# Plain fp32 state products and Newton reciprocal roots in the scan of a hybrid SSD and attention block

## The chip, the cores and the metric

The kernel runs on one core of one Trainium2 chip. The metric is the device time of one execution, in microseconds. Engines are named as in the profile: PE is TensorE, PEld its weight load, DVE is VectorE, ACT is ScalarE, POOL is GpSimd, SP is SyncE, which here only issues DMAs.

## What is computed

The reference is one encoder layer on 1024 tokens of width 1024, in float32. A combined projection feeds a bidirectional state-space scan (SSD) and a neighbourhood attention; their outputs go through one output projection and a squared-ReLU MLP. What the change touches is in these lines (cut):

```python
# ssd_chunked, once per direction, chunks of 128 tokens, 2 groups of 8 heads of 64
chunk_states = jnp.einsum("bclgn,bclgep->bcgepn", bc, xc * decay_to_end[..., None])
chunk_decay = jnp.exp(a_cum[:, :, -1])
def step(h, inp):
    s_c, d_c = inp
    return d_c[..., None, None] * h + s_c, h
_, h_in = lax.scan(step, h0, (...))
y_off = jnp.einsum("bclgn,bcgepn->bclgep", cc, h_in) * jnp.exp(a_cum)[..., None]
# ssd_mixer: gate and grouped RMSNorm over 512 columns
g = g * lax.rsqrt(jnp.mean(g * g, axis=-1, keepdims=True) + EPS)
# neighbourhood_attention: RMSNorm of q and k over each head's 64 columns
q = rmsnorm(q.reshape(bsz, t, NA_HEADS, NA_HEAD_DIM), q_norm_w) * (NA_HEAD_DIM ** -0.5)
k = rmsnorm(k.reshape(bsz, t, NA_HEADS, NA_HEAD_DIM), k_norm_w)
```

## The kernel before

The program is written tile by tile in Python; a planner orders the instructions of each engine ahead of the run, by the dependencies between tiles, the free buffers and its own estimate of each instruction's time. On the chip each engine then works through its list strictly in that order and waits, at the head of the list, for whatever is not ready.

Large products are made of three passes in a reduced fp32 format (fp32r): an operand is split into a high part, rounded by ACT, and a low part, the difference, taken by DVE or POOL; `mm3` (L177 to L180) multiplies high by high, high by low and low by high. The weights are split on their way in by `load_w` (ACT at L148, DVE or POOL at L149), values that come out of PSUM by `split_from_psum` (L184, L185; with a scale L187, L188).

The first part (up to about 275 us) norms and transposes the input (L210), projects x, B, C and dt, applies the convolution (`conv`, L448 to L484) and projects z, which goes through Silu (L509) to memory. The transposed B of each chunk is kept as split pair `bNh`, `bNl`; B and C by state row stay whole in `bT` and `cT`.

Then the scan is traced as a loop of eight steps `i` over two groups `g`, each with `backward(7 - i, g)` and `forward(i, g)`. `backward` also does the part within the chunk for both directions: C by B (`pcb`, L587), the decay matrices `rb` loaded by DMA, subtracted on POOL (L612), merged on DVE (L618), exponentiated on ACT (L623), multiplied by `pcb` on DVE (L625), and eight fp32 products `pd` on PE (L630). The outputs are added up in `y1`, on POOL (L638, L641, L649, L666) and DVE (L642). In both directions:

- `decay_state` weights x with the decay on POOL (`xw`, L653 and L672), splits it (`xh` L540 on ACT, `xl` L541 on DVE), multiplies it by the B of the chunk into `pS` (three passes), multiplies the state by its decay on POOL (L549), adds `pS` on DVE (L550) and splits the new state (`sh` L553 on ACT, `sl` L554 on DVE). `sh` and `sl` have one buffer per group, which both directions use in turn.
- `carried` splits the C of the chunk (`ch` L562, `cl` L563), multiplies it by the split state into `py` (three passes) and scales the result on DVE (`yo`, L567).
- `gated`, once per chunk and group, multiplies `y1` by the gate on DVE (L574), sums its squares on ACT (L576), takes the reciprocal root with `inv_rms`, scales on ACT (L578) and stores by a DMA from ACT's queue.

`pcb`, `pS` and `py` share two PSUM buffers ("s"); `rb` has two buffers, `yo` and `xw` one.

Behind the scan in the program, but independent of it and therefore mixed with it by the planner, stands the projection of q, k and v (`qkv_proj`, six weight blocks of eight token blocks, each 24 passes into `pq`, three PSUM buffers). For q and k `normed_split` squares on ACT (L695), sums on DVE (L697), takes the reciprocal root of 8 columns with `inv_rms`, scales on DVE (L699), transposes on PE (L705), splits (L187, L188) and stores with DMAs from ACT's queue.

`inv_rms` (L199 to L203) is two POOL instructions: mean plus epsilon (L201) and a power with the exponent -0.5 from the tile `half` (L202). It is called 32 times for q and k, 16 times in `gated`, 8 times before the MLP.

Later come the attention with the output projection mixed in (about 675 to 1050 us; L928 to L959), the MLP's first product (to about 1390 us) and its second.

## Time and profile before

| what | value |
|---|---|
| median of three runs | 1725.57 us (1724.66 to 1726.45) |
| the profiled execution | 1725.33 us |
| its span, first to last instruction | 1723.5 us |
| mean granted clock of PE | 0.98 |
| table loads of ACT, of 1283 ns each | 7, the last at 280.72 us (L623) |
| DMA traffic | 269.75 MB |

The profile is of one execution. A page of it gives busy time of each engine, the span in 40 equal slices (each digit the busy share in tenths), and the costliest groups of instructions; other views answer questions about a stretch of time, a tile or a source line, list what each engine waited for (total us, times, longest us), or the instructions in order of time (start, duration). Matmuls are pipelined, so their durations overlap and the distance between starts is what one costs. A weight load (PEld) and its matmul are two records.

### The profile page before, as it was taken

What the parts mean: (1) busy time and instruction counts of PE and PEld (TensorE: products, weight loads), DVE (VectorE), ACT (ScalarE), POOL (GpSimd) and SP (SyncE); (2) the same over time, 40 slices, a digit from 0 to 9 for tenths busy, and PEclk for the clock granted to TensorE, in tenths of its full rate; (3) what the DMA queues carried; (4) which work ended last, traced back from release to release, by engine and by line L of the source; (5) the groups of instructions that cost most, each with busy time, mean ns of one, the idle gap of its engine ahead of it and who ended that gap; (6) DMA issues with size and microseconds to landing.
All of it is one profiled execution on the core that took longest, in us unless ns stands there. A gap on an engine that the chain in (4) does not pass through costs nothing. (4 is left out here: it accounts for less than half of the span.)

```text
span 1723.5 us, 20879 instructions
## 1 busy us (share of the span) xinstructions
PE 1636.0 (95%) x7461; PEld 1304.6 (76%) x7461; DVE 1106.3 (64%) x1687; ACT 726.5 (42%) x1189; POOL 705.6 (41%) x496
## 2 busy tenths in 40 slices
PE   6999999989888999999999988999999978999999
PEld 5788888777766777777767767788888866888887
DVE  5767214889787744778787776454343359787863
ACT  5434223434344434555565533454444443333330
POOL 4000004888778741221242242244444426555551
PEclk9999999999998999999999999999999989999999
DMA  8213338876675796754453141254344394644231
GB/s 200 62 37 104 89 98 242 210 195 207 213 206 161 234 311 199 240 150 138 132 183 123 56 159 49 73 190 153 134 159 147 125 349 149 201 141 166 92 110 73
DMA packets 178499, 269.75 MB, mean 157 GB/s; under 512 B 13963, under 2 KB 105051, under 8 KB 178395
## 3 DMA queue, kind: packets, MB, share of 16 engines
q1 hardware_dynamic: 135419, 231.18, 42.6%
q10 hardware_dynamic: 42976, 37.23, 7.1%
q8 instruction: 59, 0.97, 0.2%
q14 instruction: 45, 0.37, 0.1%
HBM read 185.21 MB, written 86.50 MB: 158 GB/s over the span
## 5 line engine op out<-in xcount | busy, mean ns | idle before, releaser
L760 POOL TENSOR_TENSOR wl<-wraw,wh 128x1024 fp32r<-128x1024 f32 x110 | 300.1, 2740 | 350.1 <-ACT wh L759 336.7
L745 PE MATMUL px<-wh,ahl 128*128 128x512 f32 x512 | 163.7, 397 | 9.8 <-ACT ahl L759 9.8
L759 ACT ACTIVATE wh<-wraw 128x1024 fp32r<-128x1024 f32 x110 | 115.7, 1054 | 127.4 <-issue 42.4
L179 PE MATMUL pq<-wl,hTh 128*128 128x512 f32 x384 | 153.1, 400 | 4.6 <-DVE wl L149 4.4
L745 PE MATMUL px<-h,wh 128*128 128x512 f32 x496 | 156.5, 396 | 0.0
L178 PE MATMUL pq<-wh,hTh 128*128 128x512 f32 x384 | 153.1, 401 | 1.9 <-ACT wh L148 1.2
L180 PE MATMUL pq<-wh,hTl 128*128 128x512 f32 x384 | 151.9, 396 | 0.0
L759 ACT ACTIVATE ahl<-ar 128x1024 fp32r<-128x1024 f32 x56 | 58.9, 1053 | 173.0 <-PE px L745 89.6
L760 DVE TENSOR_TENSOR ahl<-ar,ahl 128x1024 fp32r<-128x1024 f32 x56 | 107.3, 1917 | 37.4 <-ACT ahl L759 36.2
L745 PEld LDWEIGHTS px<-wh,ahl 128*128 128x128 f32 x512 | 97.3, 190 | 31.9 <-ACT ahl L759 10.2
L745 PEld LDWEIGHTS px<-h,wh 128*128 128x128 f32 x496 | 93.4, 189 | 22.4
L149 DVE TENSOR_TENSOR wl<-wraw,wh 128x1024 fp32r<-128x1024 f32 x40 | 55.0, 1376 | 83.3 <-ACT wh L148 82.7
L878 POOL TENSOR_TENSOR mb<-braw,nam 128x256 f32<-128x256 f32 (+1 forms) x48 | 41.0, 884 | 159.7 <-DVE nmx L936 123.4
L184 ACT ACTIVATE pth<-ptp 128x384 fp32r<-128x384 f32 (+1 forms) x128 | 58.4, 459 | 107.8 <-PE ptp L959 106.8
L745 PE MATMUL px<-wl,ahl 128*128 128x512 f32 x256 | 100.9, 394 | 0.0
L745 PE MATMUL px<-h,wl 128*128 128x512 f32 x248 | 98.1, 396 | 0.0
L179 PEld LDWEIGHTS pq<-wl,hTh 128*128 128x128 f32 x384 | 73.2, 191 | 22.1 <-DVE wl L149 7.9
L149 POOL TENSOR_TENSOR wl<-wraw,wh 128x1024 fp32r<-128x1024 f32 x18 | 43.8, 2446 | 110.5 <-ACT wh L148 84.3
L745 PE MATMUL pz<-wh,ahl 128*128 128x512 f32 x256 | 82.8, 400 | 6.5 <-DVE acc L1330 5.0
L178 PEld LDWEIGHTS pq<-wh,hTh 128*128 128x128 f32 x384 | 72.9, 190 | 18.2 <-ACT wh L148 2.5
L180 PEld LDWEIGHTS pq<-wh,hTl 128*128 128x128 f32 x384 | 73.2, 191 | 14.7
L612 POOL TENSOR_TENSOR rb<-rb,c 128x512 f32<-128x512 f32 x64 | 75.0, 1192 | 21.5 <-DMA rb<-cum_dr 18.7
(265 smaller groups left out, 4242.6 us busy)
## 6 DMA issues: line engine op xcount, KB each, us to landing
act_dr<-cq SPq DMA_DIRECT2D x56, 512.0 KB, 3.0
ar<-act_dr SPq DMA_DIRECT2D x56, 512.0 KB, 3.8
wraw<-in_w_in_dram SPq DMA_DIRECT2D x44, 512.0 KB, 4.0
rb<-cum_dr SPq DMA_DIRECT2D x32, 512.0 KB, 7.6
wraw<-in_w_mlp_in_dram SPq DMA_DIRECT2D x32, 512.0 KB, 4.7
wraw<-in_w_mlp_out_dram SPq DMA_DIRECT2D x32, 512.0 KB, 5.3
q_dr<-hl ACTq DMA_DIRECT2D x64, 128.0 KB, 3.2
k_dr<-hl ACTq DMA_DIRECT2D x16, 512.0 KB, 3.2
```

Source lines behind the costliest of these rows:

```text
L149: lo_eng.tensor_tensor(lo[:, 0:n], raw[:, 0:n], hi[:, 0:n].bitcast(F32), op=sub)
L178: nc.tensor.matmul(pt, lhsT=ah, rhs=bh, start=first, stop=False)
L179: nc.tensor.matmul(pt, lhsT=ah, rhs=bl, start=False, stop=False)
L180: return nc.tensor.matmul(pt, lhsT=al, rhs=bh, start=False, stop=last)
L184: nc.scalar.activation(hi, src, AF.Copy)
L612: nc.gpsimd.tensor_tensor(rb[:, d], rb[:, d], c1[:, d, c, h0 : h0 + 4].unsqueeze(2).broadcast_to([P, 4, P]), op=sub,)
L745: nc.tensor.matmul(pt, lhsT=a, rhs=b, start=f, stop=l, skip_group_check=True)
L759: nc.scalar.activation(hl[0], src, AF.Copy)
L760: eng.tensor_tensor(hl[1], src, hl[0].bitcast(F32), op=sub)
L878: nc.gpsimd.tensor_tensor(mb[:, s].rearrange("p (s r c) -> p s r c", r=16, c=8), v[:, a:b], nam[:, s].rearrange("p (s r c) -> p s r c", r= ...
```

## The change

It has two parts. In the scan, the splits of B, of the weighted x, of the state and of C are left out, and each of the two products per chunk, group and direction is one plain fp32 matmul; the state has two buffers per direction and group and is read by PE itself; the first state of each is copied from PSUM by ACT instead of DVE. In the norms of `gated` and of q and k, `inv_rms` is replaced by a function of six instructions: mean plus epsilon on DVE, Ln and Exp with the scale -0.5 on ACT, and one Newton step in three DVE operations. An explicit instruction loads ACT's table number 6 behind the last Silu of z. The input norm and the norm before the MLP keep POOL's power.

```diff
+LN_EXP = 6
...
+    def inv_rms_newton(pool, ss, n, width, tag):
+        r = pool.tile([P, width], F32, tag=tag, name=tag, bufs=2)
+        nc.vector.tensor_scalar(ss, ss, 1.0 / n, EPS, op0=mul, op1=add)
+        nc.scalar.activation(r, ss, AF.Ln)
+        nc.scalar.activation(r, r, AF.Exp, scale=-0.5)
+        nc.vector.scalar_tensor_tensor(ss, ss, -0.5, r, op0=mul, op1=mul)
+        nc.vector.tensor_tensor(ss, ss, r, op=mul)
+        nc.vector.scalar_tensor_tensor(r, ss, 1.5, r, op0=add, op1=mul)
+        return r
...
-        bNh = sp.tile([P, NT, 2, P], F32R, name="bNh")
-        bNl = sp.tile([P, NT, 2, P], F32R, name="bNl")
+        bN = sp.tile([P, NT, 2, P], F32, name="bN")
...
-                        split_from_psum(bNh[s], bNl[s], pv)
+                        nc.scalar.copy(bN[s], pv)
...
-                    nc.scalar.activation(zs, pt, AF.Silu, scale=rcol[:, t : t + 1])
+                    last_silu = nc.scalar.activation(zs, pt, AF.Silu, scale=rcol[:, t : t + 1])
...
+            with tc.issue_after(last_silu.ins):
+                nc.scalar.add_instruction(
+                    mybir.InstLoadActFuncSet(
+                        act_func_set_id=LN_EXP,
...
             def decay_state(d, c, g, xw):
                 prev = st[d][g]
                 pS = ps_s("pS")
-                xh = qp.tile([P, 512], F32R, tag="xh", name="xh", bufs=1)
-                xl = qp.tile([P, 512], F32R, tag="xl", name="xl", bufs=1)
-                nc.scalar.activation(xh, xw, AF.Copy)
-                nc.vector.tensor_tensor(xl, xw, xh.bitcast(F32), op=sub)
-                mm3(pS, bNh[:, c, g, :], bNl[:, c, g, :], xh, xl, True, True)
-                new = prev and prev[0]
+                nc.tensor.matmul(pS, lhsT=bN[:, c, g, :], rhs=xw, start=True, stop=True)
+                new = qp.tile([P, 512], F32, tag=f"st{d}{g}", name="st", bufs=2)
                 if prev is None:
-                    new = qp.tile([P, 512], F32, tag=f"st{d}{g}", name="st", bufs=1)
-                    nc.vector.tensor_copy(new, pS)
+                    nc.scalar.copy(new, pS)
                 else:
                     dec = ed[:, d, c, 8 * g : 8 * g + 8]
-                    nc.gpsimd.tensor_tensor(h8(new), h8(new), hb(dec), op=mul)
+                    nc.gpsimd.tensor_tensor(h8(new), h8(prev), hb(dec), op=mul)
                     nc.vector.tensor_tensor(new, new, pS, op=add)
-                sh = qp.tile([P, 512], F32R, tag=f"sh{g}", name="sh", bufs=1)
-                sl = qp.tile([P, 512], F32R, tag=f"sl{g}", name="sl", bufs=1)
-                nc.scalar.activation(sh, new, AF.Copy)
-                nc.vector.tensor_tensor(sl, new, sh.bitcast(F32), op=sub)
-                st[d][g] = (new, sh, sl)
+                st[d][g] = new
...
-                ch = qp.tile([P, P], F32R, tag="ch", name="ch", bufs=2)
-                cl = qp.tile([P, P], F32R, tag="cl", name="cl", bufs=2)
-                nc.scalar.activation(ch, ct, AF.Copy)
-                nc.vector.tensor_tensor(cl, ct, ch.bitcast(F32), op=sub)
-                mm3(py, ch, cl, *st[d][g][1:], True, True)
+                nc.tensor.matmul(py, lhsT=ct, rhs=st[d][g], start=True, stop=True)
...
-                r = inv_rms(qp, ss, 512, 1, "ry")
+                r = inv_rms_newton(qp, ss, 512, 1, "ry")
...
-                r = inv_rms(hp, ss, HD, 8, "rq")
+                r = inv_rms_newton(hp, ss, HD, 8, "rq")
```

More of the change, by code (lines that the diff above doesn't have):

```diff
@@ L519, in hymba_block @@
             qp = p2.enter_context(tc.tile_pool(name="qs", bufs=2, side="right", reuse_waits="tile"))
+            with tc.issue_after(last_silu.ins):
+                nc.scalar.add_instruction(
+                    mybir.InstLoadActFuncSet(
+                        act_func_set_id=LN_EXP,
+                        name=nc.get_next_instruction_name(),
+                        engine=mybir.EngineType.Activation,
+                    )
+                )
             zt = qp.tile([P, 192], F32, tag="y1", name="zt")
```

## The prediction

> **What bounds the kernel now.** I read the page first, then the table of stretches, then the waits of TensorE and of VectorE in the one stretch where TensorE is not full, then the groups of instructions that the diff touches.
>
> ```profile
> PE 1636.0 (95%) x7461; PEld 1304.6 (76%) x7461; DVE 1106.3 (64%) x1687; ACT 726.5 (42%) x1189; POOL 705.6 (41%) x496
> ...
> PE   6999999989888999999999988999999978999999
> ...
> POOL 4000004888778741221242242244444426555551
> PEclk9999999999998999999999999999999989999999
> ```
>
> TensorE is the bound of nearly the whole span. Its longest stretch with gaps lies about the ninth to thirteenth slice (43 us each; eights among the nines), where POOL is at seven or eight tenths. This is where the scan runs, with the q, k and v projections filling TensorE between the scan's products. The stretches, with one from the attention behind it for comparison:
>
> ```profile
> 275.00:605.00 330.00, 297.61 (x1427) 237.95 (x1427) 262.32 (x382) 132.41 (x236) 263.74 (x243) 0.98 0.73 212
> 475.00:575.00 100.00, 85.81 (x384) 67.28 (x383) 80.07 (x111) 44.53 (x80) 82.10 (x77) 0.93 0.69 200
> 675.00:1000.00 325.00, 318.65 (x1542) 238.61 (x1539) 257.31 (x729) 179.22 (x448) 80.33 (x61) 0.98 0.49 153
> ```
>
> After each stretch and its length stand PE, PEld, DVE, ACT, POOL, then the granted clock. In the scan TensorE is idle for 330 - 297.6 = 32.4 us (9.8%), with DVE at 79% and POOL at 80%. In the attention DVE is at 79% too, but POOL at 25%, and TensorE is idle for 6.4 us only (2.0%). So a DVE at four fifths does not by itself starve TensorE; a POOL at four fifths beside it goes with gaps. What TensorE waits for, from 275 to 680 us, and what DVE waits for, from 275 to 605 us:
>
> ```profile
> PE pcb L587 <- DVE yo L567: 7.5, 4, 3.1
> PE pd L630 <- DVE rb L625: 7.3, 9, 1.3
> PE pq L179 <- DVE wl L149: 4.4, 5, 1.7
> PE py L178 <- DVE yo L567: 2.5, 2, 2.0
> ```
>
> ```profile
> DVE rb L618 <- POOL rb L612: 16.6, 15, 2.5
> DVE y L642 <- POOL y L641: 12.3, 6, 4.5
> DVE qn L699 <- POOL rq L202: 9.4, 14, 1.5
> DVE y L574 <- POOL y L649: 7.0, 4, 3.5
> DVE sq L697 <- ACT qn L695: 6.2, 3, 3.2
> ```
>
> TensorE waits for DVE, and DVE waits for POOL: 16.6 + 12.3 + 9.4 + 7.0 = 45 us of DVE's idle time end with a POOL operation. POOL's own queue is at the head of the chain.
>
> **The change, engine by engine.** POOL loses the reciprocal roots of the q and k norms and of the gated norms. The table of stretches, asked for the instructions that touch rq and for those that touch ry (DVE or ACT first, then POOL):
>
> ```profile
> 270.00:640.00 370.00, 23.88 (x32) 67.60 (x64) 0.98 0.77 224
> ```
>
> ```profile
> 270.00:640.00 370.00, 11.49 (x16) 17.10 (x32) 0.98 0.77 224
> ```
>
> That is 67.6 + 17.1 = 84.7 us, a third of its 263.7, and nothing is put in its place: POOL falls to about 179 us. Everything else in its queue (the rb subtractions, the y additions, st times decay, xw) moves up, and these are what DVE waits for. The product with the decay stays on POOL; it now reads the old state and writes the other buffer, at the same size.
>
> The splits go. The same table for what touches xh, sh and ch (PE, PEld, DVE, ACT); each split is one ACT and one DVE operation:
>
> ```profile
> 270.00:640.00 370.00, 23.63 (x56) 10.59 (x56) 23.12 (x28) 17.52 (x28) 0.98 0.77 224
> ```
>
> ```profile
> 270.00:640.00 370.00, 24.32 (x56) 11.34 (x56) 23.95 (x28) 17.44 (x28) 0.98 0.77 224
> ```
>
> ```profile
> 270.00:640.00 370.00, 20.92 (x56) 10.49 (x56) 13.15 (x28) 8.27 (x28) 0.98 0.77 224
> ```
>
> DVE loses 23.1 + 24.0 + 13.2 = 60 us and ACT 17.5 + 17.4 + 8.3 = 43 us. Each state product also loses an ACT step and a DVE step in front of it, and the sh and sl buffers that both directions shared. Four first states move from DVE to ACT (about 17.5/28 = 0.63 us each, by xh).
>
> DVE and ACT gain the Newton step, 48 times: four DVE operations and two ACTIVATEs on 8 columns or one. The nearest rows are the smallest ACT instruction and the scan's small DVE operation, as groups (busy us, mean ns):
>
> ```profile
> L946 ACT ACTIVATION_READ_ACCUMULATOR pr<-pr,nmx 128x1 f32 x128 | 24.2, 189 | 0.0
> ```
>
> ```profile
> L597 DVE SCALAR_TENSOR_TENSOR cf<-dt,cd,dsk 128x8 f32<-128x8 f32 x16 | 7.1, 444 | 0.3
> ```
>
> and, instruction by instruction (shortest/median/longest ns), L597 again with two large operations of DVE beside it:
>
> ```profile
> L597 DVE SCALAR_TENSOR_TENSOR cf<-dt,cd,dsk x16: 208/228/1002, 273.9 to 589.1; 128x8 f32<-128x8 f32 x16
> ```
>
> ```profile
> L618 DVE COPY_PREDICATED rb<-lmask,rb x32: 719/1560/1820, 282.4 to 596.8; 128x512 f32<-128x512 int32 x32
> ```
>
> ```profile
> L550 DVE TENSOR_TENSOR st<-st,pS x24: 665/675/682, 323.5 to 571.7; 128x512 f32<-128x512 f32 x24
> ```
>
> ACT: 96 x 0.189 to 0.299 us (the second 8.27/28 from ch, 128 columns) = 18 to 29 us, less than the 43 it loses. DVE: 192 operations between 0.208 us (shortest of L597) and 0.444 us (its mean) = 40 to 85 us. The two ends differ for a reason that the last two rows show: the state addition L550, with one input in PSUM, always takes 0.67 us, while L618, with both in SBUF, takes from 0.72 to 1.82 us, mostly 1.56; L597, whose operands are all in SBUF, is stretched to 1.0 us at times. I put the stretch down to POOL, which is busy beside them 80% of the time. With POOL down from 80% to 56% of the stretch (179 of about 320 us) I scale the excess: 0.208 + 0.236 x 56/80 = 0.373 us, and 192 x 0.373 = 72 us. DVE then stands at 262 - 60 + 72 = 274 us before the rest of its two-input operations get shorter for the same reason (L618 alone has up to 32 x (1.56 - 0.72) = 27 us of excess): about 265 us, no better and no worse than before.
>
> The Trainium skill (SBUF — State Buffer, Who interferes with whom) gives the rule that speaks against this change: a VectorE instruction with two SBUF inputs and a GpSimd instruction that reads SBUF exclude one another for a whole instruction, whichever came first. By that rule three of the four Newton operations can each be held for the rest of a POOL operation, and the price would be nearer the 85 us than the 40, which with the same relief elsewhere takes the time some 3 us up, to about 1717; the rows of L550 and L618 agree with it.
>
> Waits that the change adds: DVE's second operation of the Newton step sits in DVE's queue until ACT's Exp is done, and behind it stand rb, yo and st of the scan, for which TensorE waits; Ln sits in ACT's queue until DVE's first operation is done, and behind it stand the rb Exps and the DMA issues of q, k, v and y. Bounds: a handoff from ACT to DVE costs DVE now 6.2 us in the 28 reductions of the stretch (sq behind qn), 0.22 us each, so 48 x 0.22 = 11 us; the same for POOL's rq, which goes, is 9.4 us. They cancel. The chain of one norm (67.6/32 = 2.1 us on POOL) becomes 4 x 0.373 + 2 x 0.2 = 1.9 us with two more handoffs; three PSUM buffers of pq cover it, and without them it would be about a microsecond each.
>
> TensorE: 28 pS and 28 py products, three fp32r passes each, become one fp32 product. The trace has a product of that size and type, prr (L324, ones times dg); each is recorded as two instructions:
>
> ```profile
> 47.52 0.39 PE L178 MATMUL px<-hTh,wh 128*128 128x512 f32 x1
> 47.74 0.39 PE L179 MATMUL px<-hTl,wh 128*128 128x512 f32 x1
> 47.97 0.40 PE L180 MATMUL px<-hTh,wl 128*128 128x512 f32 x1
> 48.20 1.02 PE L324 MATMUL prr<-dg,cst 128*128 128x512 f32 x2
> 48.66 0.80 PE L178 MATMUL px<-hTh,wh 128*128 128x512 f32 x1
> 49.30 0.39 PE L179 MATMUL px<-hTl,wh 128*128 128x512 f32 x1
> ```
>
> Starts tell the pitch, as durations overlap: three passes take 48.20 - 47.52 = 0.68 us; from 48.20 to 49.30 there is one fp32 product and one pass of 0.23 us, so the product takes 0.87 us. The difference, 0.19 us x 56 = **+10.6 us** of TensorE work, lies on the bound and is hidden by nothing.
>
> Edits at no cost: bN as one copy drops four DVE subtractions about 57 to 100 us, where the slices of TensorE show 9; the table load that stood in front of the first rb Exp stands behind the last Silu instead.
>
> **The sum.** TensorE's idle time after the change: by POOL's share alone, between the attention (25%, 2.0%) and the scan (80%, 9.8%), 56% gives 6.4%, or 20 us of some 320; at the attention's rate it would be 6 us. I take 13, midway, since POOL's share leaves out the 56 places where a product no longer waits for ACT and DVE. That is 32.4 - 13 = **-19 us**. The clock of 0.93 from 475 to 575 us costs 7 us and stands where the gaps are thickest (14 of 100 us), but the attention has 0.98 with few gaps, so I count **-3** (ends 0 and -7). Sum: 10.6 - 19 - 3 = -11 us. The profiled execution took 1725.33 us (span 1723.5), 0.2 us from the median of the runs, so 1714 us stands for both. Its own ends: idle 6 us and the clock back, 10.6 - 26 - 7 = -22, 1703; idle 20 us, clock restored by half, 10.6 - 12 - 3 = -4, 1721.
>
> **Rivals.** *It cancels.* POOL's relief gives 12 us back (idle 20) and the clock nothing: 1725.3 + 10.6 - 12 = 1724. For it: the interpolation taken plainly; the two largest waits of TensorE end with yo and rb on DVE, and the two largest of DVE with rb and y on POOL, operations that all stay. Against: they stand in a shorter POOL queue.
>
> *DVE takes POOL's place, slower.* DVE's instructions in the stretch grow from 382 by 192 - 88, and each Newton step holds its queue for ACT, whose queue is held by DMA issues. At 85 us for the step and none of the relief DVE is at 262 - 60 + 85 = 287 us, 87% of 330, and waits for ACT come on top. Then TensorE's gaps stay at 32 us, and the fp32 products are all that is seen: 1725.3 + 10.6 = 1736; with 1 us for each of the 48 handoffs, a quarter of it passed on, 1748. It decides from a DVE share of about 85% on. Against: the attention runs at 79% with almost no gap, and handoffs from ACT have cost 0.22 us.
>
> *The table is not what the change wants.* Before the scan one Ln and the Exp behind it each had a load of their own:
>
> ```profile
> 119.95 1.28 ACT L416 ACT_TABLE_LOAD   x1
> 121.24 0.42 ACT L416 ACTIVATE c<-c 128x256 f32<-128x256 f32 x1
> 121.68 1.28 ACT L410 ACT_TABLE_LOAD   x1
> ```
>
> If the explicit load does not hold one table for both, 48 norms pay up to two loads, 96 x 1.28 = 123 us of ACT, in the middle of a chain on which DVE waits; with a fifth of it passed on to TensorE, 1725 + 25 = 1750. The Trainium skill (ScalarE: Activation LUTs, Table sets: the hidden batching unit) names a set that has both functions, which would make this 0; no run here shows it.
>
> **How the numbers follow.** Runs of this kernel can tell some 0.2%, 3.5 us, from no change: faster is under 1722, slower over 1729. Forecast (1703 to 1721): 0.55, and 0.04 for more than that. It cancels: 0.16. DVE takes POOL's place: 0.22. The table: 0.03. Faster 0.59, same 0.16, slower 0.25. The range, 1702 to 1736, leaves out the worse half of the third case, the last and what lies below the forecast.
>
> **What would show it.** Right: in the scan POOL near 180 us; TensorE's idle time near 13 us and the waits of pd and pcb halved; 112 fp32 matmul instructions at L324's pitch; DVE's waits for rb and y of POOL down by half; one table load after 270 us. Wrong: L618 and the Newton operations as stretched as before, DVE above 85% of the scan, TensorE's wait for yo or rb as long or longer, new waits of DVE for the Exp of the norm above 20 us, or tables loaded in the scan. A granted clock that stays at 0.93 would take 3 us of the gain.

## The result, and the profile after

The changed kernel takes 1745.92 us, median of four runs (1744.93 to 1751.01), beside 1726.01 us for the kernel before on the same chip (1724.66 to 1727.24): a ratio of 1.012, interval 1.0104 to 1.0136. It is slower by some 20 us, where 11 us less had been forecast. The profiled execution took 1745.74 us, with a span of 1743.7.

The page of the changed kernel, the lines that answer to those shown of before:

```profile
PE 1649.8 (95%) x7405; PEld 1298.9 (74%) x7405; DVE 1093.6 (63%) x1787; ACT 710.9 (41%) x1205; POOL 612.7 (35%) x400
...
PE   6999999999888899999999988999999978999999
...
POOL 4000003665664311212222342144444426555551
PEclk9999999999999999999999999999999989999999
```

POOL lost 93 us over the whole span, and its digits in the scan went from sevens and eights to fives and sixes. TensorE's eights did not go; there are as many as before (four in the scan), later. The stretches of the changed kernel (each with PE, PEld, DVE, ACT, POOL, then the granted clock):

```profile
275.00:605.00 330.00, 298.07 (x1315) 221.59 (x1313) 244.73 (x446) 107.73 (x229) 183.73 (x159) 0.95 0.72 212
475.00:575.00 100.00, 86.64 (x364) 63.93 (x364) 71.43 (x148) 36.84 (x86) 51.55 (x43) 0.91 0.67 201
675.00:1000.00 325.00, 317.89 (x1529) 238.94 (x1528) 249.29 (x712) 177.98 (x438) 82.69 (x62) 0.98 0.50 155
```

POOL fell from 264 to 184 us in the scan, DVE from 262 to 245 (74%), ACT from 132 to 108. Every engine that feeds TensorE is less busy, and TensorE has the same 32 us of gaps (330 - 298.1), at a lower clock: 0.95 instead of 0.98, and 0.91 instead of 0.93 in the middle. What TensorE and DVE waited for, in the changed kernel:

```profile
PE py L569 <- DVE st L563: 8.0, 6, 4.2
PE pd L635 <- DVE rb L630: 7.8, 3, 6.3
PE pq L180 <- DVE wl L150: 4.0, 5, 2.0
PE py L569 <- DVE yo L572: 3.5, 3, 1.9
...
PE pcb L592 <- DVE yo L572: 2.4, 2, 2.0
```

```profile
DVE rb L623 <- POOL rb L617: 46.8, 18, 7.9
...
DVE sq L211 <- ACT rq L210: 1.5, 3, 0.5
```

TensorE's wait for yo is smaller than before (5.9 us instead of 10.0 by these lists) and the one for rb as long in sum, but in fewer and longer pieces (6.3 us at once, before 1.3 at most), and the wait for the state addition `st` has become the largest. DVE waits for POOL's `rb` for 46.8 us instead of 16.6; it waits for the Exp of a norm hardly at all.

To see where the time goes I added up the starts and ends of all matmuls from 270 us to the last `pq`. Each distance from one start to the next is split into the gap (no matmul running), the time lost because the granted clock was below full, and the rest, the work at full clock:

| kernel | gaps, us | lost to the clock, us | work, us | last pq at | attention's last score product (psc) at |
|---|---|---|---|---|---|
| before | 33.0 | 6.4 | 361.2 | 670.6 | 981.9 |
| changed | 35.1 | 15.6 | 366.7 | 687.5 | 1003.2 |

Up to the last `pq` the change costs 16.9 us: 2.1 of gaps, 9.2 of clock and 5.5 of work. The attention behind it adds 4 us more up to its last score product, the rest of the span nothing that matters. The column of work is the least sure: waits that are shorter than the overlap of two matmuls count as work, and over the kernels tried below that have the same matmuls it scatters by 5 to 7 us. The forecast's terms for the three were -19, -3 and +10.6.

The longest gaps are followed by a lower clock. TensorE from a gap of 4.20 us on in the changed kernel (start, duration; the distances between starts count), and the same on DVE just ahead of it:

```profile
541.35 0.39 PE L181 MATMUL pq<-wh,hTl 128*128 128x512 f32 x1
545.93 2.07 PE L569 MATMUL py<-st,cT 128*128 128x512 f32 x2 [4.20 <-DVE st L563]
...
549.08 0.63 PE L180 MATMUL pq<-wl,hTh 128*128 128x512 f32 x1
549.51 0.63 PE L181 MATMUL pq<-wh,hTl 128*128 128x512 f32 x1
...
551.22 0.63 PE L179 MATMUL pq<-wh,hTh 128*128 128x512 f32 x1
551.64 0.48 PE L180 MATMUL pq<-wl,hTh 128*128 128x512 f32 x1
```

```profile
541.96 0.73 DVE L623 COPY_PREDICATED rb<-lmask,rb 128x512 f32<-128x512 int32 x1 [3.67 <-POOL rb L617]
542.58 0.14 DVE L208 TENSOR_SCALAR ss<-ss 128x1 f32<-128x1 f32 x1
542.64 1.17 DVE L211 SCALAR_TENSOR_TENSOR sq<-sq,rq 128x8 f32<-128x8 f32 x1
543.84 0.17 DVE L212 TENSOR_TENSOR sq<-sq,rq 128x8 f32<-128x8 f32 x1
543.92 0.68 DVE L702 TENSOR_REDUCE sq<-qn 128x8 f32<-128x512 f32 x1
544.52 0.16 DVE L213 SCALAR_TENSOR_TENSOR rq<-sq,rq 128x8 f32<-128x8 f32 x1
544.59 0.68 DVE L579 TENSOR_TENSOR y<-y,sz 128x512 f32<-128x512 f32 x1
545.20 0.68 DVE L563 TENSOR_TENSOR st<-st,pS 128x512 f32<-128x512 f32 x1
```

After the gap the passes start 0.43 us apart (549.08, 549.51) until 551.6, where they stood 0.23 apart before; so a gap of 4.2 us costs nearly 3 us more behind it (5.7 us at half clock). And the state addition that ends it stands in DVE's queue behind a late `rb` (DVE had been idle for 3.67 us until POOL had it), the first operation of a gated norm, the three Newton operations of a q or k norm (one of them 1.17 us long), a reduction and a product with the gate. By the starts, the Newton operations hold 1.35 us of this gap; in the longest gap, 6.32 us before the `pd` at 477.54, it is 2.33 us (L211 to L213 from 471.87 to 474.20), again behind a late `rb`. In these two gaps the Newton operations are a part, and the late `rb` stands ahead of them. Of the gaps longer than 2 us before the last `pq`, the kernel before has two (5.7 us in sum), the changed kernel six (19.4 us).

### The profile page after: what moved, and what is told of

Same layout as the page of the kernel before. It is cut to its first block, busy times and chain, and to the rows that moved or that the text cites. A ratio compares the mean times of both kernels' runs of the same rounds, so it can differ in the third digit from the quotient of the medians.

```text
span 1743.7 us, 20748 instructions
## 1 busy us (share of the span) xinstructions
PE 1649.8 (95%) x7405; PEld 1298.9 (74%) x7405; DVE 1093.6 (63%) x1787; ACT 710.9 (41%) x1205; POOL 612.7 (35%) x400
## 5 line engine op out<-in xcount | busy, mean ns | idle before, releaser
L180 PE MATMUL pq<-wl,hTh 128*128 128x512 f32 x384 | 160.8, 420 | 4.2 <-DVE wl L150 4.0
L179 PE MATMUL pq<-wh,hTh 128*128 128x512 f32 x384 | 158.8, 417 | 0.0
L765 DVE TENSOR_TENSOR ahl<-ar,ahl 128x1024 fp32r<-128x1024 f32 x56 | 110.6, 1977 | 35.1 <-ACT ahl L764 33.9
L750 PEld LDWEIGHTS px<-wh,ahl 128*128 128x128 f32 x512 | 97.2, 190 | 32.1 <-ACT ahl L764 10.1
L617 POOL TENSOR_TENSOR rb<-rb,c 128x512 f32<-128x512 f32 x64 | 72.9, 1161 | 44.1 <-DMA rb<-cum_dr 43.2
```

The costliest lines, as they stand in the source:

```text
L179: nc.tensor.matmul(pt, lhsT=ah, rhs=bh, start=first, stop=False)
L180: nc.tensor.matmul(pt, lhsT=ah, rhs=bl, start=False, stop=False)
L617: nc.gpsimd.tensor_tensor(rb[:, d], rb[:, d], c1[:, d, c, h0 : h0 + 4].unsqueeze(2).broadcast_to([P, 4, P]), op=sub,)
L750: nc.tensor.matmul(pt, lhsT=a, rhs=b, start=f, stop=l, skip_group_check=True)
L765: eng.tensor_tensor(hl[1], src, hl[0].bitcast(F32), op=sub)
```

## The experiments

The theories at the start: A, the fp32 products' extra TensorE work is the loss; B, the Newton norms are; C, `rb` comes too late by DMA. For what inside the norms costs: D, the time of their small operations on DVE; H, the trip of the chain through ACT and back; R, that the planner writes another order of the queues for every changed list of instructions, and that this alone moves the time. Two were added on the way: O, ScalarE's additional instructions cost by holding its queue; Q, what costs is that the norm's instructions stand in the queues of DVE and ACT at all. Gaps, clock and last `pq` are added up as in the table above, from the one execution of each kernel that was profiled. Ratios are against the kernel before, run on the same chip.

**The two halves.** The products alone are the changed kernel with POOL's power in all norms:

```diff
-                r = inv_rms_newton(qp, ss, 512, 1, "ry")
+                r = inv_rms(qp, ss, 512, 1, "ry")
...
-                r = inv_rms_newton(hp, ss, HD, 8, "rq")
+                r = inv_rms(hp, ss, HD, 8, "rq")
```

> The change without its norms: fp32 state products and whole operands as in the changed kernel, all norms with POOL's power as before. Theory A (TensorE pays: 56 products x 0.19 us = 10.6 us, and long gaps in front of them lower the granted clock): about 1740 us or more, since the gaps come with the products; clock loss (length of a stretch x (1 - granted clock), summed from 275 to 725 us) above 12 us. Theory B (the Newton step on VectorE and ScalarE makes the long gaps): 1736 us or less, only the 10.6 us of the products seen, clock loss near the 7 us of the kernel before. Theory C (the new order waits longer for the DMA of rb, whichever part brings it): no forecast for this run.

Measured: 1.0042 (1.0027 to 1.0057), 7 us; gaps 26.8, clock 13.1: the time is as B had it, the loss to the clock (13.7 us in the sum from 275 to 725 us that the expectation names) as A had it. The Newton half alone is the kernel before with the opposite edit and the table load:

> The kernel before with the Newton norms (q, k and gated) and the explicit table load alone; splits and three-pass products stay. Theory A: no slower than before, 1715 to 1728 us, since POOL loses 85 us and TensorE's work is unchanged. Theory B: slower, 1735 us or more, with VectorE above 85% of the scan (192 small operations on top of the splits) and a clock loss above 12 us. Theory C: POOL's wait for the DMA of rb grows from 18.7 us to some 40 us, as in the changed kernel.

Measured: 1.0068 (1.0053 to 1.0083), 12 us; gaps 43.9, clock 10.5, with DVE at 291.7 of 330 us (88%). Time, load and clock (13.7 us from 275 to 725 us) are as B had them; POOL's wait for the DMA of `rb` is 32.1 us, short of C's 40. The halves add up to the 20 us, and the norms are the larger one. But with POOL still at 77% (254.7 of 330 us) the first has fewer gaps than the changed kernel with POOL at 56%, and the second, with POOL at 59%, has more than the kernel before. POOL's share does not order them.

**The products' form.** The changed kernel with three fp32r passes for each product, over unsplit operands (so the products come out three times too large, over rounded operands):

```diff
-                nc.tensor.matmul(pS, lhsT=bN[:, c, g, :], rhs=xw, start=True, stop=True)
+                mm3(pS, bN[:, c, g, :], bN[:, c, g, :], xw, xw, True, True)
...
-                nc.tensor.matmul(py, lhsT=ct, rhs=st[d][g], start=True, stop=True)
+                mm3(py, ct, ct, st[d][g], st[d][g], True, True)
```

> The changed kernel, but each of the 56 state products is three fp32r passes over the same unsplit operands instead of one fp32 matmul (B, C, the weighted x and the state are kept rounded to fp32r; the products come out three times too large, so the outputs are not the reference's). TensorE's work is that of the kernel before, nothing is split, the norms are the Newton ones. Theory A: the 10.6 us of the products go, and if the products themselves make the gaps, all of it: 1724 to 1736 us. Theory C: only the 10.6 us go, the gaps and a clock loss near 19 us stay: about 1735 us.

Measured: 1.0066 (1.0041 to 1.0091); work 354.1 us. Against the changed kernel, 12.6 us less work and some 9 us less time. The gaps stay at 36.0 us and the clock's loss is 19.5 us, so the fp32 products are not what makes the gaps. The size of the prediction's product term stands, within the scatter of the work column. In the changed kernel itself one product takes 0.86 us, from its start to the next one's:

```profile
489.75 1.02 PE L556 MATMUL pS<-xw,bN 128*128 128x512 f32 x2
490.61 0.38 PE L592 MATMUL pcb<-cT,bT 128*128 128x128 f32 x2
```

**The late rb.** The longest wait in the list of DVE, 46.8 us for POOL's `rb`, itself waits for a DMA. A third buffer for it:

```diff
-                    rb = qp.tile([P, 2, 4, P], F32, tag="rb", name="rb", bufs=2)
+                    rb = qp.tile([P, 2, 4, P], F32, tag="rb", name="rb", bufs=3)
```

> The changed kernel with three buffers for rb instead of two. Theory C (POOL waits 43 us for the DMA of rb, which waits for a buffer, and the longest gaps of TensorE stand behind that chain): POOL's wait for rb falls under 20 us, the gap of 6.3 us goes, the clock loss falls by half, 1730 to 1738 us. Theories A and B: no more than 3 us off the changed kernel's 1746.

Measured: 1.0119 (1.0101 to 1.0137), no change. POOL's wait for the DMA of `rb` did not change either: 43.6 us, 43.2 in the changed kernel. Theory C falls in the form that a buffer more would help; what the late `rb` costs is not shown, as no run takes that wait away. The longest wait of a list need not be the one that counts: DVE in the fastest version below still waits 39.0 us there. The run also bears on R. From 275 to 660 us VectorE executes the same 511 instructions in both kernels, but their order parts at the 33rd, and the time is the same: another order by itself need not move it.

**Parts of the norms, beside the splits.** Without the three Newton operations (Ln and Exp stay):

```diff
-        nc.vector.scalar_tensor_tensor(ss, ss, -0.5, r, op0=mul, op1=mul)
-        nc.vector.tensor_tensor(ss, ss, r, op=mul)
-        nc.vector.scalar_tensor_tensor(r, ss, 1.5, r, op0=add, op1=mul)
```

> The kernel before with Ln and Exp for the norms, but without the Newton step: mean plus epsilon on VectorE, then Ln and Exp on ScalarE (the root keeps their error). Against the Newton norms alone (1736.7 us, VectorE 292 of 330 us busy) it takes 144 small VectorE operations away and keeps every handoff to and from ScalarE. Theory D (the Newton operations fill VectorE's queue, on which TensorE waits): 1722 to 1729 us, VectorE near 255 us, TensorE's gaps from 44 back to 33 us or fewer. Theory H (a norm now waits in ScalarE's queue behind DMA issues and other work): 1733 us or more.

Measured: 1.0047 (1.0028 to 1.0065), 3.6 us less than with them, a difference no larger than the two intervals leave open; the time is as H had it, with DVE at 279.1 us. With the new norm in q and k only, and POOL's power in the gated norms:

> The kernel before with the Newton norms for q and k alone (32 of the 48); the gated norms keep POOL's power. TensorE's transposes of q and k wait behind these norms, the gated ones end in a DMA. Theories D and H, if the q and k chain is what TensorE feels: most of the 11 us of the Newton norms, 1732 to 1738 us. If the gated norms are what counts (their ScalarE and SyncE queue hold loads): 1729 us or less.

Measured: 1.0126 (1.0101 to 1.015), worse than with all 48 changed, and above both ranges expected. With the mean and a reciprocal on DVE, and nothing on POOL or ACT (square root left out):

```diff
+        nc.vector.tensor_scalar(ss, ss, 1.0 / n, EPS, op0=mul, op1=add)
+        nc.vector.reciprocal(r, ss)
```

> The kernel before with the 48 norms wholly on VectorE: mean plus epsilon and a reciprocal, two small operations (the square root is left out, so the output is not the reference's). POOL loses its 85 us, no handoff to ScalarE, 96 small operations on VectorE (about 20 us). It is the step of the prediction by itself that POOL's load makes TensorE's gaps. If that step holds: gaps near 20 us, 1710 to 1716 us. If POOL's load is not what TensorE waits for: 1722 to 1730 us, gaps near 33 us.

Measured: 0.9984 (0.9969 to 0.9998), as said for the case that POOL's load is not what TensorE waits for. The table of stretches for it:

```profile
275.00:605.00 330.00, 302.62 (x1454) 242.85 (x1453) 275.02 (x474) 135.72 (x240) 188.68 (x160) 0.98 0.73 214
```

POOL is relieved just as in the changed kernel (188.7 us), with a norm of two small DVE operations (DVE 275.0 us, 262.3 before), and TensorE's busy time rises by 5 us only; the time falls by 3 us. That is all that POOL's relief is worth beside the splits with this norm in its place. The table load by itself, as a control:

> The kernel before with nothing but the explicit table load behind the last Silu; all splits, products and norms as before. What a new plan by itself can do: the planner orders every engine anew. If small changes leave the plan alone: within 2 us of before. Theory R (part of the 6 and 11 us of the two halves is a matter of the plan, not of the work): it moves by 3 us or more, either way.

Measured: 1.0012 (0.9997 to 1.0028): nothing that can be told from no change. The planner left the order nearly as it was (460 of VectorE's 462 instructions from 265 to 690 us stand in the same sequence), so this run does not test R.

**The same instructions, off the chain.** The next two start from the reciprocal and put the other instructions behind it, over the finished sum, where nobody reads their result (the first has the table load as well):

```diff
         nc.vector.reciprocal(r, ss)
+        nc.scalar.activation(ss, ss, AF.Ln)
+        nc.scalar.activation(ss, ss, AF.Exp, scale=-0.5)
```

> The kernel before, with the norms' root replaced by mean plus epsilon and a reciprocal on VectorE (the square root is left out, so the output is not the reference's), as in the run that took 0.998 of before; behind it, off the chain, ScalarE still computes Ln and Exp into the finished sum, which nobody reads. It has the same ScalarE and VectorE instructions as the kernel with Ln and Exp without a Newton step (1.0047), plus one small reciprocal, but nobody waits for ScalarE's result. Theory H (the price of Newton is the wait for ScalarE inside the chain of a norm): the wait is gone, so 0.998 to 1.000 of before, 1722 to 1727 us. Theory O (ScalarE's 96 instructions themselves, by holding its queue): 1.004 to 1.006, 1733 to 1736 us, as with them in the chain. Theory R (the order that the planner writes differs, and that alone is worth up to 10 us): anywhere from 0.997 to 1.010, and TensorE's gaps between 270 us and the last pq anywhere from 27 to 45 us without a new wait that ends on ScalarE.

Measured: 1.0026 (1.0005 to 1.0047), between what H and O gave, so inconclusive; R's range of 0.997 to 1.010 holds it, as it would hold nearly any result here. Nobody reads the result, but the queue is not free of waiting: ACT stands for 32.1 us in front of the Ln of q and k until DVE's reciprocal is done. With the three DVE operations in place of Ln and Exp:

> The same kernel with the reciprocal (square root left out, output not the reference's), and behind it, off the chain, the three Newton operations on VectorE over the finished sum, which nobody reads. So the 144 small VectorE operations by themselves, without a wait for ScalarE. Theory D (VectorE's time is the price): 144 x 0.31 us = 45 us more in its queue, VectorE at 88% or more of the scan, and a good part of the 11.7 us that all of Newton cost: 1.003 to 1.006, 1731 to 1736 us. Theory H (the wait for ScalarE): no wait, so 0.998 to 1.001, 1722 to 1728 us.

Measured: 1.0038 (1.0022 to 1.0053), 9 us over the reciprocal alone, with DVE at 294.7 of 330 us (89%), both as D had it:

```profile
275.00:605.00 330.00, 299.52 (x1421) 240.95 (x1420) 294.74 (x588) 134.67 (x237) 190.80 (x157) 0.97 0.72 210
```

So, beside the splits, the operations cost by standing in DVE's queue, with nobody waiting for their result. Then the new norm in the gated norms alone, with POOL's power for q and k:

> The kernel before with the Newton norm only in the 16 gated norms; q and k keep GpSimd's power. Newton in all 48 cost 1.0068, in the 32 of q and k alone 1.0126. Theory H or D (each norm has its price): a third of 11.7 us or less, 1.001 to 1.003, 1728 to 1731 us. If prices simply added, all 48 less the 32 would be a gain of 10 us, 1716 us, which would be a kernel faster than both; theory R (the order decides) allows this, and any time from 1716 to 1740 us, with no relation to the number of norms changed.

Measured: 1.0055 (1.0035 to 1.0076), more than H or D had. The two runs that change a part of the norms cost 22 and 9 us, the run that changes all of them 12: beside the splits the prices do not add, which R allows.

**The changed kernel, taken apart.** The changed kernel with the reciprocal norm:

> The changed kernel with the reciprocal on VectorE in place of the Ln, Exp and Newton step (square root left out, output not the reference's): fp32 products, GpSimd relieved, no wait for ScalarE in a norm. If the parts add, the products (1.0042) and the reciprocal (0.998) give 1.0025, 1730 us. By the prediction's reason (GpSimd's load makes TensorE's gaps) both reliefs together should give the gaps of 13 us that it forecast, and with them 1714 to 1720 us. Theory H: the whole difference to the changed kernel, some 15 us, is the price of the six-instruction norm: 1728 to 1733 us. Theory R: TensorE's gaps within 27 to 45 us, and the time not the sum of the parts by 5 us or more.

Measured: 1.0013 (0.9993 to 1.0033), gaps 21.4, clock 11.5, work 366.0. The time lies between what the prediction's reason gave (1714 to 1720 us) and what H gave (1728 to 1733), and the parts of the two halves add up to it within the interval (1.0025). Here the gaps do fall, to what the prediction's interpolation by POOL's share gave (20 us); the products with POOL's power had 26.8 and 1.0042, so beside the fp32 products POOL's relief is worth some 5 us. Some 18 us of the loss come from Ln, Exp and Newton in place of the reciprocal. All of these put behind the reciprocal, where nobody reads their result:

> The changed kernel with a reciprocal on VectorE in the chain of each norm (square root left out, output not the reference's), and all of the rest of the six-instruction norm, three VectorE operations, Ln and Exp, behind it over the finished sum, where nobody waits for it. The same kernel without that rest took 1.0013 of before, the changed kernel 1.012. Theory Q (what costs is that the instructions stand in the queues of VectorE and ScalarE at all): 1.008 to 1.012, 1740 to 1746 us, TensorE's gaps up to the last pq at 32 us or more. Theory H (what costs is that the chain of a norm goes through ScalarE and back, with two handoffs): 1.001 to 1.004, 1727 to 1733 us, gaps near the 21 us of the kernel without the rest.

Measured: 1.0049 (1.0031 to 1.0067), gaps 30.3, between what Q and H gave. By the differences, 6 us are for standing in the queues, and the other 12 us of the changed kernel for standing in the chain. The queues are again not free of waiting: ACT stands for 41.6 us in front of the Ln of q and k until DVE has done the operations ahead of it. The root as two ACT instructions, without any DVE operation (epsilon comes from an added ninth column of `half`):

```diff
-        nc.vector.tensor_scalar(ss, ss, 1.0 / n, EPS, op0=mul, op1=add)
-        nc.scalar.activation(r, ss, AF.Ln)
+        nc.scalar.activation(r, ss, AF.Ln, scale=1.0 / n, bias=half[:, 8:9])
         nc.scalar.activation(r, r, AF.Exp, scale=-0.5)
-        nc.vector.scalar_tensor_tensor(ss, ss, -0.5, r, op0=mul, op1=mul)
-        nc.vector.tensor_tensor(ss, ss, r, op=mul)
-        nc.vector.scalar_tensor_tensor(r, ss, 1.5, r, op0=add, op1=mul)
```

> The changed kernel with the norms' root as two instructions of ScalarE alone: Ln with the mean as its scale and epsilon as its bias, and Exp with the scale -0.5; no VectorE operation. In the gated norm the chain stays on ScalarE from the square to the scaling. Theory Q: VectorE loses 192 operations of 0.31 us (60 us), only 96 small ScalarE operations stay: most of the 19 us come back, 1.001 to 1.004, 1727 to 1733 us. Theory H: one handoff from VectorE and one back remain for q and k, none in the gated norm: about half comes back, 1.005 to 1.008, 1734 to 1740 us.

Measured: 1.0014 (1.0 to 1.0029), gaps 22.3. Q's expectation holds. The changed kernel with the stores of q, k and v issued by GpSimd:

```diff
-                            nc.scalar.dma_start(
+                            nc.gpsimd.dma_start(
```

> The changed kernel with the stores of q, k and v issued from GpSimd's queue instead of ScalarE's (one such issue stood for 5.64 us in front of an Exp that the gated norm's VectorE step waited for). If the long waits for the Exp and Ln behind these issues carry the slowdown, 1.003 to 1.008, 1731 to 1740 us, and the longest gap of TensorE before the last pq falls under 4 us. If the number of instructions carries it, no change or worse, since GpSimd's queue, where rb and the y additions stand, then holds the issues: 1.010 to 1.018, 1743 to 1757 us.

Measured: 1.008 (1.0052 to 1.0108). The scan gains (last `pq` at 666.8 instead of 687.5, longest gap 3.6 us), but the attention gives half of it back: its last score product ends at 992.5, 326 us after the last `pq` instead of 316. The time is at the upper end of the first case. It fits that waits behind DMA issues on ACT are part of the loss in the scan, and that moving them to another queue moves some of it; as the order changes too, it does not show it. (The 5.64 us are three issues in a row, not one.) The changed kernel without the three Newton operations, Ln and Exp kept in the chain (the edit of the run beside the splits):

> The changed kernel without the three VectorE operations of the Newton step; Ln and Exp stay in the chain, and the step before them on VectorE. Beside splits and three passes the three operations cost 3.6 us (1.0068 against 1.0047). Theory H (the trip through ScalarE): 1.008 to 1.011, 1739 to 1745 us. Theory Q (instructions in the queues; three of the four VectorE operations are gone): 1.003 to 1.007, 1731 to 1738 us.

Measured: **0.9956 (0.9939 to 0.9972)**, 1719.96 us median, faster than both kernels; both theories had expected a smaller gain. Its table of stretches, and what TensorE and DVE wait for:

```profile
275.00:605.00 330.00, 308.20 (x1400) 233.60 (x1399) 220.75 (x347) 116.03 (x255) 185.20 (x160) 0.98 0.77 232
475.00:575.00 100.00, 89.92 (x401) 66.71 (x399) 72.92 (x117) 44.52 (x102) 53.70 (x44) 0.97 0.71 211
```

```profile
PE ptq L707 <- DVE qn L701: 9.0, 4, 4.6
PE pd L632 <- issue: 3.1, 1, 3.1
PE pd L632 <- DVE rb L627: 3.1, 5, 1.1
```

```profile
DVE rb L620 <- POOL rb L614: 39.0, 21, 8.3
...
DVE qn L701 <- ACT rq L210: 7.4, 11, 1.8
```

TensorE's gaps are 330 - 308.2 = 21.8 us, its clock is back at 0.98 and at 0.97 in the middle, and the wait for `st` is gone. DVE does wait for the Exp now, 7.4 us, and the time shows no price for it: here the trip through ACT is not what costs. Last, Newton left out of the 16 gated norms only, and of the 32 norms of q and k only:

> The changed kernel with the three VectorE operations of the Newton step left out of the 16 gated norms and kept in the 32 of q and k. All 48 steps took 1.012, none 0.9956. Theory Q (each step has its price in the queues): a third of the 28 us comes back, 1.006 to 1.008, 1736 to 1740 us. Theory R (the order that the planner writes for this very list of instructions is the cause): a time not in proportion to the number of steps, from 0.995 to 1.015, and this run and its counterpart, with the step left out of q and k, do not add up to the 28 us.

> The counterpart: the three Newton operations kept in the 16 gated norms, left out of the 32 of q and k. Theory Q: two thirds of the 28 us come back, 1.000 to 1.002, 1725 to 1730 us. Theory R: any time from 0.995 to 1.015, with what the two runs give back summing to less than 18 us or more than 38 us instead of 28.

Measured: 1.0062 (1.0045 to 1.0078) and 1.0014 (1.0 to 1.0027). The first gives back 1.012 - 1.0062 = 0.0058, the second 0.0106, in sum 0.0164; leaving out all 48 gives back 1.012 - 0.9956 = 0.0164. So in the changed kernel the Newton steps have a price that adds up, as Q had it: 28 us over 48, some 0.6 us each, 10 us for 16 and 18 us for 32. That the sums agree to the last digit is chance: each ratio is known to some 0.0015, and by the medians it is 11 + 18 us against 26. For this list of instructions R is not needed, but not excluded either, since leaving the steps out also reorders the rest (VectorE's other instructions from the first norms on, at 287.6 us).

| kernel | ratio | gaps | clock | last pq at |
|---|---|---|---|---|
| changed, reciprocal | 1.0013 | 21.4 | 11.5 | 668.9 |
| changed, reciprocal, rest off the chain | 1.0049 | 30.3 | 8.4 | 675.4 |
| changed, Ln and Exp on ACT alone | 1.0014 | 22.3 | 8.0 | 660.4 |
| changed, no Newton | 0.9956 | 21.8 | 5.6 | 662.1 |
| changed, Newton in gated only | 1.0014 | 24.3 | 6.2 | 665.1 |
| changed, Newton in q and k only | 1.0062 | 30.8 | 7.7 | 675.5 |
| changed | 1.012 | 35.1 | 15.6 | 687.5 |

Among the last four kernels the last column rises with the number of Newton steps (0, 16, 32, 48). The times of some of these kernels scatter by some 10 us from run to run, so differences of 0.002 between single ratios shouldn't be read as differences, and the sums, from one execution each, less still: "Newton in gated only" was profiled at 1721.86 us, where its median is 1728.17.

## Why the prediction was wrong

**The products, +10.6: right in size, about.** One product takes 0.86 us in the changed kernel, 0.87 was read. Three passes in its place take off 12.6 us of work and 9 us of time. Between the kernels the work rose by 5.5 us only, with a scatter as large as that, and the products with POOL's power cost 7 us, less what the missing splits gave back.

**TensorE's idle time, -19: the step that failed.** "TensorE's idle time after the change: by POOL's share alone" took POOL as what makes the gaps, and the DVE operations that come in its place as free, since DVE's total would be "no better and no worse than before". POOL fell as forecast (184 us, 179 said; of the 84.7 us taken off, read from 270 to 640 us, 74.6 lie in the stretch), and DVE fell further (245 us, 265 said), but the gaps stayed at 32 in the stretch. Three comparisons say why. POOL's relief beside the splits is worth 3 us (reciprocal), with gaps of 27.4 us in the stretch at a POOL share of 57%. With the splits gone the gaps are 21 to 22 us (reciprocal, no Newton), near the 20 of the plain interpolation; that is partly luck, since the same POOL share beside the splits does not give it. And the Newton operations put the gaps back: 35 with all 48, 31 with 32, 24 with 16, 22 with none. The operations' own time is what was read, or less; the groups of the changed kernel (busy us, mean ns), for q and k:

```profile
L211 DVE SCALAR_TENSOR_TENSOR sq<-sq,rq 128x8 f32<-128x8 f32 x32 | 11.6, 363 | 3.1 <-ACT rq L210 3.0
...
L213 DVE SCALAR_TENSOR_TENSOR rq<-sq,rq 128x8 f32<-128x8 f32 x32 | 10.2, 320 | 0.6
...
L212 DVE TENSOR_TENSOR sq<-sq,rq 128x8 f32<-128x8 f32 x32 | 8.6, 269 | 0.4
```

A step's three operations are 0.36 + 0.27 + 0.32 = 0.95 us of DVE, and 0.6 us of that reach the end of the kernel. An engine at four fifths (74% in the event) was taken to have room for them. But DVE works through its list in order, and what TensorE waits for (`st`, `rb`, `qn`) stands behind whatever small operation comes first, as in the two longest gaps. The share of busy time doesn't show this. The prediction also set the chain of one norm at the operations' own time, 2.1 us before and 1.9 after. From the end of a q or k norm's reduction to the start of its scaling (L702 to L704) the mean is 5.1 us in the kernel before, 5.4 in the changed kernel and 3.5 without Newton: 2 us more for 0.95 us of work, which fits that each of the three operations takes its own place between others in the queue. The length of this chain by itself does not order the kernels, though: with Newton in q and k only it is 5.7 us at 1.0062, with everything behind the reciprocal 2.4 us at 1.0049. (The small ACT operation read from ch is 8.27/28 = 0.295 us, not 0.299; nothing hangs on it.)

**The clock, -3: wrong sign, +9.** The term was tied to the sum of the gaps, and that does not give it: gaps of 33.0 and 35.1 us go with 6.4 and 15.6 us of clock. Nor does the number of long gaps, though the changed kernel has six over 2 us where there were two: the reciprocal beside the splits also has six (14.5 us in sum) and loses 6.4 us, the products alone have three (8.7 us) and lose 13.1. What sets it stays open. The clock gave back 10 of the 25 us by which the last `pq` came earlier when the Newton operations left (15.6 to 5.6 us).

**Stretched operations.** The forecast scaled the excess of DVE's two-input operations by POOL's share. The changed kernel's rows (shortest/median/longest ns; L211 from 270 to 640 us, 30 of the 32):

```profile
L623 DVE COPY_PREDICATED rb<-lmask,rb x32: 716/1546/1830, 282.2 to 592.5; 128x512 f32<-128x512 int32 x32
L211 DVE SCALAR_TENSOR_TENSOR sq<-sq,rq x30: 140/166/1251, 287.3 to 632.6; 128x8 f32<-128x8 f32 x30
```

The merge of `rb` is as long as before (1.55 us, 1.56 before) with POOL at 56%, so the 27 us of excess didn't shrink; "L618 as stretched as before" was one of the signs named for being wrong, and it came. A Newton operation is 0.17 us mostly and up to 1.25 at times. By the Trainium skill (SBUF — State Buffer, Who interferes with whom), a VectorE operation with two SBUF inputs and a GpSimd instruction that reads SBUF shut each other out for a whole instruction; the longest rows fit it. The 85 us that the prediction put beside that rule for the 192 operations of the norms on DVE did not come: they took 60.1 us in all.

**The rivals.** "DVE takes POOL's place" gave 1736 to 1748 and the gaps at 32 us, and both came so. Its mechanism did only in part: it was to decide from a DVE share of 85% on, and DVE stood at 74%; its handoffs were to cost 1 us each, and DVE waited 1.5 us in the whole stretch for the Exp of q and k and 1.2 us for that of the gated norms. Where its condition is met, in the Newton half alone (88%), the gaps are 43.9 us. In the changed kernel it is DVE's queue, by what stands in it ahead of TensorE's operands rather than by its load; that step is read from two gaps and the price per Newton step, and no run isolates it from the order. "The table" didn't come: one load lies behind 270 us (1.28 us at 270.15), none in the scan behind it, and the load alone cost nothing (both traces have eight loads; the seven in the table of the kernel before is one short). "It cancels" is the changed kernel with the reciprocal, at 1.0013.

**What stays open.** Beside the splits, the same three operations cost 3.6 us in the chain and 9 us off it, instead of 28, and the prices of 16, 32 and 48 changed norms are 9, 22 and 12 us. The order that the planner writes for each list is the only thing that could differ that I know of, but no run holds the order and changes the instructions; the one run that holds the instructions and changes the order (the third buffer) left the time as it was. What the late `rb`, ahead of both longest gaps, costs by itself was not tested. Whether the 12 us between the norm's instructions in the chain and beside it are the longer chain or such an order, is open too. And the parts differ by kernel: in the changed kernel, Ln and Exp in the chain are faster than a reciprocal (0.9956 against 1.0013) though they do more, which no theory here had.

## What to carry to other kernels

A small operation on an engine that works in order isn't free because the engine is idle a quarter of the time: ask what stands behind it in the queue, and who waits for that. Where one engine is relieved by loading another with more, shorter instructions in a dependent chain, count the chain's places in the queue beside the busy time; here each step of 0.95 us went with a chain longer by 2 us and a kernel longer by 0.6. Leaving the refinement out, where the accuracy of Ln and Exp is enough, turned a loss of 1.2% into a gain of 0.4%.

## What the runs showed of the hardware

After an idle time of TensorE of 3 us or more the granted clock is nearly always halved for several microseconds, after 2 to 3 us often. I counted the gaps in the profiles of all 20 kernels, from 270 us to the last `pq`, behind which half clock is running or begins within 3.5 us: 32 of 33 gaps of 3 us or more, 37 of 57 of 2 to 3 us, 32 of 130 of 1 to 2 us. In the changed kernel a gap of 2.01 us that ends at 519.82 is followed by half clock, another of 2.01 us that ends at 500.76 is not, and half clock also comes, from 350.43 to 353.84, with no gap over 0.9 us near it. In the kernel before, a gap of 3.12 us is followed by passes 0.43 us apart for some 3 us:

```profile
497.94 0.77 PE L587 MATMUL pcb<-cT,bT 128*128 128x128 f32 x2 [3.12 <-DVE yo L567]
...
500.21 0.63 PE L178 MATMUL pq<-wh,hTh 128*128 128x512 f32 x1
500.64 0.63 PE L179 MATMUL pq<-wl,hTh 128*128 128x512 f32 x1
...
501.34 0.39 PE L178 MATMUL pq<-wh,hTh 128*128 128x512 f32 x1
501.57 0.39 PE L179 MATMUL pq<-wl,hTh 128*128 128x512 f32 x1
```

In the changed kernel it was 5.7 us after a gap of 4.20 us. The Trainium skill (TensorE: Matmul & The Clock Gate, Part 1: The HAM clock gate) puts it at about 3.4 us of sustained work until the full clock returns; the first place agrees (granted clock 0.50 for 3.41 us, from 497.73 to 501.14), the second took twice that (6.83 us, from 544.99 to 551.82). So a long gap mostly costs more than its own length, and several short ones of the same sum often do not, which a sum of idle times doesn't tell.
